# The attention scores' second product with the queries' high parts alone, the key blocks on two halves of the array's rows

## The chip, the cores and the metric

The kernel runs on one core of a Trainium2 chip. A core has TensorE (PE, the matrix array; its weight loads are listed apart as PEld), VectorE (DVE), ScalarE (ACT), GpSimd (POOL) and SyncE (SP, which here only issues transfers), and 16 DMA engines. The metric is the device time of one execution in microseconds; less is better.

## The reference, cut to what matters

One layer of a diffusion backbone over 1024 latent tokens and 256 context tokens, 1024 wide: a token mixer (a gated recurrence beside grouped-query attention), then a mixture of 16 experts. The change is in the attention alone: 8 query heads of 64 numbers, 2 key heads, each shared by 4 query heads, 1280 keys.

```
xqa = apply_axial_rope(rms_norm(heads(xaq, 8), q_norm_g), cos, sin)      # queries, (1, 1024, 8, 64)
keys = jnp.concatenate([cka, xka], axis=1)                                # (1, 1280, 2, 64)
...
s = jnp.einsum("bqhgd,bkhd->bhgqk", qi, k) * 64 ** -0.5                   # one block of 128 queries
p = jax.nn.softmax(s, axis=-1)
o = jnp.einsum("bhgqk,bkhd->bqhgd", p, v)
```

## The kernel before

All matrix products are of float32 numbers, and each number is kept as two parts: a high part rounded to the width that the array multiplies (`fp32r`), and a low part, the rest. A product is then a sum of products of parts. `split` makes both parts, the high one on ACT (line 92) and the low one on DVE (line 93).

The instructions of PE stand in the order in which the program is written; those of the other engines and of SP's queue are put in order by a scheduler, which follows priorities. Each engine runs its own in order.

**The attention** (lines 709 to 933) goes over 16 pairs (t, g): a tile t of 128 queries and a key head g with its 4 query heads. For each pair, 24 steps put on PE, in turn: `turn` (line 801: a block of the probabilities of this pair is turned, 4 transposes on line 804, then split), `softmax` of one head of the next pair (line 776), some matmuls of independent work (`fill.run`: the gates' projections, later the first branch, lines 176 to 178), and `values` (line 809: two matmuls on line 814). So while one pair is turned and multiplied with the values, the next one's scores are made. The amount of independent work at each step is fixed when the program is written.

**The scores.** `q_vec(t)` (line 743) norms and rotates a tile of queries on DVE (the first two tiles) or POOL (the others), with tables `cq` and `sq` that stay on the chip, and `q_turn(t)` (line 763) puts them on the array's rows: a tile `QT[t, g]` holds for each head 128 rows, the 64 high parts and under them the 64 low parts. The keys `KT[g]` have the two parts side by side along the free dimension, each one twice on the rows: `KT[g][:, 0]` is the high parts on rows 0 to 63 and again on rows 64 to 127, `KT[g][:, 1]` the low parts in the same way. So one matmul over 128 rows with `KT[g][:, 0]` gives (high + low of the query) times the key's high part, and a second one with `KT[g][:, 1]` adds (high + low of the query) times the key's low part. The 1280 keys are three blocks of 512, 512 and 256 (`SEG`), so a head takes 6 matmuls over all 128 rows. Behind each block's second matmul DVE takes the block's maximum over the keys (line 788); behind the third, line 792 joins the three, and ACT makes the exponentials (line 795). There are three banks `s` for scores (`NS`).

At the start of the attention PE has 16 us of independent work by the program's own count (`F0`), then `q_turn(0)` and the first four heads, with 3.4 us of independent work (`F1`) after each.

After the attention come the two branches' products and the output projection (from line 937), the routing of tokens to experts (from line 1185) and the experts, whose weights stream in from memory.

Of the kernel before, what the change touches and what calls it, by code (L numbers as in the profile page):

```python
# [28 lines left out]
def view(t, off, dims):  # L29
    """The tile's partitions with free dimensions [stride, size] from element off on."""  # L30
    a = t if isinstance(t, bass.AP) else t[:]
    return bass.AP(tensor=a.tensor, offset=a.offset + off, ap=[list(a.ap[0])] + [list(d) for d in dims])
# [13 lines left out]
def _layer(tc, nc, top, A, out):  # L46
# [35 lines left out]
    def rsqrt(pool, ss, n, scale, name):  # L82
        """(ss * scale + eps) ** -0.5"""
        m = pool.tile([128, n], F32, name=name + "m", tag="rsm", bufs=4)
        nc.gpsimd.tensor_scalar(m, ss, scale, EPS, op0=OP.mult, op1=OP.add)
        r = pool.tile([128, n], F32, name=name, tag="rsr", bufs=4)
        nc.gpsimd.tensor_tensor(r, m, mhalf[:, :n], op=OP.pow)
        return r

    def split(hi, lo, src, eng=None):  # L90
        """hi: src rounded to the parts' width; lo: what is left (exact)."""
        nc.scalar.copy(hi, src)  # L92
        (eng or nc.vector).tensor_tensor(lo, src, hi.bitcast(F32), op=OP.subtract)  # L93
# [3 lines left out]
    class Fill:  # L97
        """Matmuls of independent work, emitted between the steps of a dependent chain: the time is the tensor engine's."""
# [27 lines left out]
        def flushed(self):  # L126
            """The PSUM bank is on its way out: no matmuls into it for some steps."""
            self.wait = self.pause
# [7 lines left out]
    class Stream:  # L136
        """The weight chunks of the first sub-layer in the order of their use; each is loaded one chunk ahead."""
# [18 lines left out]
    def wload(src, kt, ncols, rowlen, off, hl=None):  # L156
        """A chunk of a weight: kt row tiles of 128, ncols columns from off on; as hi and lo."""
        raw = wp.tile([128, 2048], F32, name="raw", tag="raw", bufs=1)
        if not hl:
            hl = [wp.tile([128, 2048], F32R, name="w" + x, tag="w%s%d" % (x, nw[0] % 2)) for x in ("hi", "lo")]  # L160
            nw[0] += 1
        hi, lo = hl
        f = lambda t: t.rearrange("p (k c) -> p k c", k=kt)
        nc.sync.dma_start(f(raw), dram(src, off, [[rowlen, 128], [128 * rowlen, kt], [1, ncols]]))
        split(f(hi), f(lo), f(raw))
        return f(hi), f(lo)
# [5 lines left out]
    def mm3g(p, a, b, nk, first=True, last=True):  # L172
        """p += sum over k of a[k].T @ b[k]; a, b: pairs of functions of k giving the hi and lo parts."""
        for k in range(nk):
            s, e = first and k == 0, last and k == nk - 1
            nc.tensor.matmul(p, a[0](k), b[0](k), start=s, stop=False)  # L176
            nc.tensor.matmul(p, a[0](k), b[1](k), start=False, stop=False)  # L177
            nc.tensor.matmul(p, a[1](k), b[0](k), start=False, stop=e)  # L178
            yield 3 * p.shape[-1] / 2400

# [8 lines left out]
    # the tokens, halves of them apart: [half][hi, lo]  # L189
# [15 lines left out]
    def natural(hi, lo, emit, tiles):  # L205
        """Token rows on the partitions: emit(token tile, PSUM); ctx tiles are 0, 1, x tiles 2 to 9."""
        n = hi.shape[2]
        for t in tiles:
            h = HC if t < 2 else HX[(t - 2) // 4]
            o = (t if t < 2 else (t - 2) % 4) * 128  # L210
            p = pjt()
            yield from mm3g(p[:, :n], (lambda k: h[0][:, k, o:o + 128], lambda k: h[1][:, k, o:o + 128]),
                            (lambda k: hi[:, k], lambda k: lo[:, k]), 8)
            emit(t, p[:, :n])
            fill.flushed()

    def transposed(hi, lo, m, emit, ctx, halves=(0, 1)):
        """Features on the partitions: emit(first token, number of tokens, PSUM)."""
# [23 lines left out]
    with ExitStack() as st:  # L242
# [11 lines left out]
        # token tile t is loaded, normalised and transposed beside these row tiles of w_mod (9: after them)  # L254
# [51 lines left out]
        # rows 0, 1: the products with the hi parts of silu(c), silu(c_ctx); rows 2, 3: with the lo parts  # L306
# [64 lines left out]
    def rope_swap(o, x, s, eng):  # L371
        """o = x with the halves of each axis exchanged, times s; [128, heads, 64] each."""
        for i in range(2):
            u = lambda a, j: a.rearrange("p h (a f) -> p h a f", a=2)[:, :, :, j * 16:j * 16 + 16]
            eng.tensor_tensor(u(o, i), u(x, 1 - i), u(s, i), op=OP.mult)

    def gain_rows(rows, n):
        """A head's gains on all partitions, and the same with the halves of each axis exchanged."""
# [8 lines left out]
    lbp = consts.tile([128, 2, 4], F32, name="lbp")  # L387
    lb1 = consts.tile([128, 2, 4], F32, name="lb1")
    with ExitStack() as st:
        pool = st.enter_context(mkpool("right", name="sa", bufs=2))  # L390
        pps = st.enter_context(mkpool(name="saps", bufs=1, space=PSUM))
        # lower bounds: a softmax over the two layers' logits, its first component
# [19 lines left out]
        # keys: norm, rotary embedding; values as they are  # L412
# [63 lines left out]
        # the other adaLN parameters, as one row  # L476
# [33 lines left out]
        # their sums over the partitions, piece j of 512 on row j  # L510
# [20 lines left out]
    with ExitStack() as st:  # L531
# [41 lines left out]
        for i in range(2):  # L573
            for c in range(4):
                # of the last chunk the first half of the tokens first: it makes room
# [53 lines left out]
        def states(h, K, Z, acc, tt):  # L629
# [17 lines left out]
            def advance(d, i0, cs, kt):  # L647
# [3 lines left out]
                for i, c in enumerate(cs):  # L651
# [4 lines left out]
                    else:  # L656
                        # the state before the next chunk
# [51 lines left out]
    sOA = spill.tile([4, 128, T], F32, name="sOA")  # L709
    sBA = spill.tile([8, 128, T], F32, name="sBA")  # L710
    BA, BR, direct = [], [], [None]
# [6 lines left out]
    with ExitStack() as st:  # L718
# [15 lines left out]
        cq = pool.tile([128, 8, 64], F32, name="cq")  # L734
        sq = pool.tile([128, 8, 64], F32, name="sq")
        for i, (n, a) in enumerate((("c_cos", cq), ("c_sin", sq))):
            nc.scalar.dma_start(a, A[n].rearrange("(t p) c -> p t c", p=128))
            (nc.gpsimd, nc.vector)[i].tensor_tensor(a, a, rows[:, i:i + 1].to_broadcast([128, 8, 64]), op=OP.mult)
        QT, SC = {}, {}
# [3 lines left out]
        def q_vec(t):  # L743
            eng = nc.vector if t in QV else nc.gpsimd
            x = pool.tile([128, 8, 64], F32, name="aq", tag="aq")
            nc.sync.dma_start(x, sAQ[t].rearrange("p (h d) -> p h d", h=8))
            a = pool.tile([128, 8, 64], F32, name="qa", tag="qa")
# [8 lines left out]
            eng.tensor_tensor(a, x, cq[:, t:t + 1].to_broadcast([128, 8, 64]), op=OP.mult)  # L756
            rope_swap(b, x, sq[:, t:t + 1].to_broadcast([128, 8, 64]), eng)
# [14 lines left out]
        PT, SU = {}, {}  # L772
# [3 lines left out]
        def softmax(t, g, h):  # L776
            if h == 0:
                SU[t, g] = pool.tile([128, 3, 4], F32, name="su", tag="su", bufs=3)
            m = pool.tile([128, 8], F32, name="m", tag="m", bufs=3)
# [3 lines left out]
            for a, (c0, n, _) in enumerate(SEG):  # L783
                s = ps.tile([128, 512], F32, name="s", tag="s", bufs=NS)[:, :n]
                for i in range(2):
                    nc.tensor.matmul(s, QT[t, g][:, h], KT[g][:, i, c0:c0 + n], start=(i == 0), stop=(i == 1))  # L786
                with tc.high_priority(offset=HP):
                    nc.vector.tensor_reduce(m[:, a:a + 1], s, axis=AX.X, op=OP.max)  # L788
                ss.append(s)
            hp = tc.high_priority(offset=HP)  # L790
# [59 lines left out]
        def branch_in():  # L850
            """The first half of the tokens makes room for the first branch's input."""
# [90 lines left out]
    with ExitStack() as st:  # L942
# [4 lines left out]
        # the router on x1: its weights take the norm's gain and the scale; the shift gives a row  # L947
# [21 lines left out]
        # merged branches: [hi, lo][row tiles 0-3, 4-7][tokens 0-511, 512-1023]  # L969
# [95 lines left out]
        def y_part(t, c, nc_):  # L1065
            """x1 = x + g1 * y, quarters c, ... of the columns; their part of the mean square."""
# [49 lines left out]
        def spread(t):  # L1116
            """Tile t's affinities with (expert, copy) on the partitions: ar, and the top halves of the words in ar16."""
# [16 lines left out]
        def after(t, c):  # L1134
            """What follows the matmuls of quarter c of tile t."""
# [44 lines left out]
    with ExitStack() as st:  # L1180
        pool = st.enter_context(mkpool(name="tk", bufs=1))
        ps = st.enter_context(mkpool(name="tkps", bufs=1, space=PSUM))
        # token numbers and gates as exact parts
# [7 lines left out]
        # bits of the threshold from the top, 3 a round: the first 4 rounds on the words' top halves as numbers;  # L1191
        # float32 numbers hold the threshold exactly for 8 rounds, the last 6 bits are put in as bits
# [62 lines left out]
        # counted from 1: the rank among the larger, and after all of those the rank among the equal  # L1255
# [12 lines left out]
    with ExitStack() as st:  # L1268
# [39 lines left out]
        def chunk(src, e, n, kh):  # L1308
# [4 lines left out]
            # the low half goes where an earlier chunk came from  # L1313
# [28 lines left out]
        with tc.high_priority(offset=1000):  # L1342
            route(0)
            # the tensor engine stays busy, and its clock up, while the first tokens are gathered
# [6 lines left out]
        for e in range(16):  # L1351
# [36 lines left out]
            # the last expert meets the other experts' sums on chip; the final norm follows tile by tile  # L1388
# [106 lines left out]
```

## Time and profile before

| | us |
|---|---|
| median of 3 runs | 1856.06 (1855.23 to 1858.42) |
| span of the profiled execution | 1854.5 |
| PE busy in the span | 1731.6 (93%) |
| DVE busy | 1331.0 (72%) |
| ACT busy | 995.4 (54%) |
| POOL busy | 273.7 (15%) |

The span runs from the first instruction to the last one of the profiled execution; the median lies 1.6 us above it. Times inside the program are given in microseconds from the span's start. A matmul's record is longer than the time until the next one can start, because matmuls follow each other in a pipeline; so the cost of one on PE is read from the distance of two starts, and PE's busy time is an upper bound. A form such as `24*128` behind MATMUL or LDWEIGHTS is the size of the weights, rows by columns. The attention is the stretch from about 633 us to 1012 us.

### The profile page before, as it was taken

To read this page: it belongs to the slowest core of one execution; us is meant where nothing else is said; L and a number is where in the kernel's file an instruction comes from. 1 tells how busy PE (TensorE), PEld (TensorE's weight loads), DVE (VectorE), ACT (ScalarE), POOL (GpSimd) and SP (SyncE) were. 2 spreads that over 40 slices of the span, in tenths; PEclk is the share of its full clock that TensorE was granted. 3 is DMA by queue.
4 is the path that set the end of the run, shared out by engine and by line. 5 is a ranking of instruction groups with operands and counts; after the bars stand their busy time and mean duration, and the time that the engine had idled before them with its cause. 6 is when DMAs were issued, how large, how long until landed. Compare 5 with 4: busy or idle time off the path is not lost. (4 is left out here: it accounts for less than half of the span.)

```text
span 1854.5 us, 26192 instructions
## 1 busy us (share of the span) xinstructions
PE 1731.6 (93%) x9820; PEld 1454.9 (78%) x9820; DVE 1331.0 (72%) x2000; ACT 995.4 (54%) x1632; POOL 273.7 (15%) x241
## 2 busy tenths in 40 slices
PE   5899999999999799999999999939999999999995
PEld 2798887899988678787787788828888888887774
DVE  6656323876766466777875664469999999998897
ACT  6422331322323367777876532227777777777665
POOL 3400001020000201111100332140011001001103
PEclk9899999999999999999999999959999999999998
DMA  8285445353332410101212776459999999999972
GB/s 326 93 309 208 171 140 198 106 174 103 103 117 81 130 43 29 46 29 58 89 51 87 261 262 238 159 187 358 378 379 371 379 379 374 376 379 379 370 261 101
DMA packets 206319, 383.87 MB, mean 207 GB/s; under 512 B 17488, under 2 KB 65568, under 8 KB 202864
## 3 DMA queue, kind: packets, MB, share of 16 engines
q1 hardware_dynamic: 194944, 360.92, 54.4%
q0 software_dynamic: 4832, 19.34, 3.8%
q10 hardware_dynamic: 6416, 1.94, 0.4%
q8 instruction: 77, 1.26, 0.3%
q14 instruction: 50, 0.41, 0.1%
HBM read 323.02 MB, written 59.13 MB: 206 GB/s over the span
## 5 line engine op out<-in xcount | busy, mean ns | idle before, releaser
L93 DVE TENSOR_TENSOR elo<-eraw,ehi 128x1024 fp32r<-128x1024 f32 x378 | 452.2, 1221 | 22.2 <-ACT ehi L92 14.4
L92 ACT CAST ehi<-eraw 128x1024 fp32r<-128x1024 f32 x384 | 383.6, 1047 | 86.6 <-PE pgu L178 48.5
L177 PE MATMUL pgu<-elo,xeT 128*128 128x512 f32 x512 | 203.7, 398 | 2.8 <-DVE elo L93 2.4
L176 PE MATMUL pgu<-ehi,xeT 128*128 128x512 f32 x512 | 204.9, 400 | 0.2 <-ACT xeT L92 0.2
L178 PE MATMUL pgu<-ehi,xeT 128*128 128x512 f32 x512 | 202.4, 395 | 0.0
L176 PE MATMUL pj<-hx,whi 128*128 128x512 f32 x448 | 185.4, 414 | 6.5 <-ACT stg L69 5.3
L178 PE MATMUL pj<-hx,wlo 128*128 128x512 f32 x448 | 175.8, 392 | 0.0
L177 PE MATMUL pj<-hx,whi 128*128 128x512 f32 x448 | 175.5, 392 | 0.0
L795 ACT ACTIVATE p<-s,m,qsc 128x512 f32<-128x512 f32 (+1 forms) x192 | 134.3, 713 | 17.7 <-DVE m L792 17.5
L788 DVE TENSOR_REDUCE m<-s 128x1 f32<-128x512 f32 (+1 forms) x192 | 104.3, 596 | 48.5 <-PE s L786 48.2
L176 PE MATMUL pj<-whi,hx 128*128 128x256 f32 x448 | 130.9, 292 | 3.6 <-DVE stg L541 1.9
L92 ACT CAST pT<-ptp 128x512 fp32r<-128x512 f32 x160 | 92.7, 595 | 71.9 <-PE ptp L804 71.8
L178 PE MATMUL pj<-whi,hx 128*128 128x256 f32 x448 | 128.1, 286 | 1.4 <-DVE hx L93 1.3
L93 DVE TENSOR_TENSOR pT<-ptp,pT 128x512 fp32r<-128x512 f32 x160 | 108.3, 685 | 29.2 <-ACT pT L92 28.5
L177 PE MATMUL pj<-wlo,hx 128*128 128x256 f32 x448 | 127.4, 284 | 0.0
L177 PEld LDWEIGHTS pgu<-elo,xeT 128*128 128x128 f32 x512 | 96.3, 188 | 29.0 <-DVE elo L93 8.0
L176 PEld LDWEIGHTS pgu<-ehi,xeT 128*128 128x128 f32 x512 | 96.9, 189 | 21.8 <-ACT xeT L92 0.5
L178 PEld LDWEIGHTS pgu<-ehi,xeT 128*128 128x128 f32 x512 | 96.2, 188 | 22.6 <-DVE xeT L93 0.4
L1385 POOL DMA_INDIRECT ACC<-ye,idx x15 | 34.7, 2316 | 474.9 <-DVE ye L1384 474.9
L176 PE MATMUL pye<-ehi,hdT 128*128 128x512 f32 x256 | 104.8, 409 | 0.0
L177 PE MATMUL pye<-elo,hdT 128*128 128x512 f32 x256 | 102.1, 399 | 1.2 <-DVE elo L93 1.2
L814 PE MATMUL pv<-pT,vs 128*128 128x512 f32 x320 | 102.2, 403 | 0.9 <-DVE pT L93 0.8
(365 smaller groups left out, 3919.7 us busy)
## 6 DMA issues: line engine op xcount, KB each, us to landing
eraw<-in_w_exp_gate SPq DMA_DIRECT2D x64, 1024.0 KB, 12.0
eraw<-in_w_exp_up SPq DMA_DIRECT2D x64, 1024.0 KB, 11.6
eraw<-in_w_exp_down SPq DMA_DIRECT2D x64, 1024.0 KB, 12.2
wm<-in_w_mod SPq DMA_DIRECT2D x24, 1024.0 KB, 6.9
raw<-in_w_in SPq DMA_DIRECT2D x21, 1024.0 KB, 6.1
sFK<-sg SPq DMA_DIRECT2D x32, 256.0 KB, 2.3
sGT<-stg SPq DMA_DIRECT2D x32, 256.0 KB, 2.1
sgm<-sGT SPq DMA_DIRECT2D x32, 256.0 KB, 3.8
```

Source lines behind the costliest of these rows:

```text
L92: nc.scalar.copy(hi, src)
L93: (eng or nc.vector).tensor_tensor(lo, src, hi.bitcast(F32), op=OP.subtract)
L176: nc.tensor.matmul(p, a[0](k), b[0](k), start=s, stop=False)
L177: nc.tensor.matmul(p, a[0](k), b[1](k), start=False, stop=False)
L178: nc.tensor.matmul(p, a[1](k), b[0](k), start=False, stop=e)
L788: nc.vector.tensor_reduce(m[:, a:a + 1], s, axis=AX.X, op=OP.max)
L795: nc.scalar.activation(p, ss[a], AF.Exp, bias=m[:, 7:8], scale=sc, accum_out=SU[t, g][:, a, h:h + 1])
L814: nc.tensor.matmul(PV[t, g].rearrange("p a b -> p (a b)"), VS[:, g, j], hl[i], start=(j == 0 and i == 0), stop=(j == 9 and i == 1))
L1385: nc.gpsimd.indirect_dma_start(out=ACC, out_offset=bass.IndirectOffsetOnAxis(ap=idx[:, :1], axis=0), in_=ye, in_offset=None, compute_op=OP ...
```

## The change

The second product (the key's low parts) keeps the queries' high parts alone; the queries' low part times the key's low part is left out. It then has 64 rows in place of 128. The first two key blocks' second products are put on different halves of the array's rows: block 0 on rows 0 to 63, block 1 on rows 64 to 127, one right behind the other. Block 2 takes rows 0 to 63 by itself. For block 1 the queries' high parts must lie on rows 64 to 127: a new tile `Q2[t, g]` gets them from `QT[t, g]` by a transfer of 128 KB on SP's queue, one for each of the 16 pairs. In the built program the 192 second products are matmuls over half the rows (64 by 128), 128 of them at row 0 and 64 at row 64; the 192 first products stay at 128 by 128.

The room for `Q2` comes from the rotary tables: they are no longer kept on the chip. They are scaled as before, written to a table `sRT` in memory once, and `q_vec(t)` loads its 128 rows of both (`cs`, 64 KB) each time.

```diff
+    sRT = spill.tile([8, 128, 2, 64], F32, name="sRT")
...
-        cq = pool.tile([128, 8, 64], F32, name="cq")
-        sq = pool.tile([128, 8, 64], F32, name="sq")
-        for i, (n, a) in enumerate((("c_cos", cq), ("c_sin", sq))):
+        for i, n in enumerate(("c_cos", "c_sin")):
+            a = pool.tile([128, 8, 64], F32, name="rt", tag="pT1", bufs=3)
             nc.scalar.dma_start(a, A[n].rearrange("(t p) c -> p t c", p=128))
             (nc.gpsimd, nc.vector)[i].tensor_tensor(a, a, rows[:, i:i + 1].to_broadcast([128, 8, 64]), op=OP.mult)
+            nc.sync.dma_start(sRT[:, :, i].rearrange("t p c -> p t c"), a)
...
+            cs = pool.tile([128, 2, 64], F32, name="cs", tag="cs")
+            nc.sync.dma_start(cs, sRT[t])
...
-            eng.tensor_tensor(a, x, cq[:, t:t + 1].to_broadcast([128, 8, 64]), op=OP.mult)
-            rope_swap(b, x, sq[:, t:t + 1].to_broadcast([128, 8, 64]), eng)
+            eng.tensor_tensor(a, x, cs[:, :1].to_broadcast([128, 8, 64]), op=OP.mult)
+            rope_swap(b, x, cs[:, 1:].to_broadcast([128, 8, 64]), eng)
...
+                Q2[t, g] = pool.tile([128, 4, 128], F32, name="q2", tag="q2", bufs=2)
+                nc.sync.dma_start(Q2[t, g][64:], QT[t, g][:64].bitcast(F32))
...
-                for i in range(2):
-                    nc.tensor.matmul(s, QT[t, g][:, h], KT[g][:, i, c0:c0 + n], start=(i == 0), stop=(i == 1))
-                with tc.high_priority(offset=HP):
-                    nc.vector.tensor_reduce(m[:, a:a + 1], s, axis=AX.X, op=OP.max)
+                nc.tensor.matmul(s, QT[t, g][:, h], KT[g][:, 0, c0:c0 + n], start=True, stop=False)
                 ss.append(s)
+                if a == 0:
+                    continue
+
+                for b in ((0, 1) if a == 1 else (2,)):
+                    c1, n1, _ = SEG[b]
+                    r = slice(64, 128) if b == 1 else slice(0, 64)
+                    nc.tensor.matmul(ss[b], (Q2[t, g][r, h].bitcast(F32R) if b == 1 else QT[t, g][r, h]), KT[g][r, 1, c1:c1 + n1], start=False, stop=True)
+                    with tc.high_priority(offset=HP):
+                        nc.vector.tensor_reduce(m[:, b:b + 1], ss[b], axis=AX.X, op=OP.max)
```

The order on PE at the first head before (buffer numbers kept, so that the three banks `s` can be told apart):

```order
L769 MATMUL ptq_5507<-identr_78,qs_5409 128x128 x4
L786 MATMUL s_5515<-kT_5353,qT_5499 128x512 x2
L786 MATMUL s_5519<-kT_5353,qT_5499 128x512 x2
L786 MATMUL s_5523<-kT_5353,qT_5499 128x256 x2
L176 MATMUL pj_5543<-hx_83,whi_5275 128x512
```

The same place now; line 791 is the first product, over 128 rows, and line 799 the second, over 64:

```order
L773 MATMUL ptq_5512<-identr_78,qs_5414 128x128 x4
L791 MATMUL s_5522<-kT_5354,qT_5504 128x512
L791 MATMUL s_5524<-kT_5354,qT_5504 128x512
L799 MATMUL s_5522<-kT_5354,qT_5504 128x512
L799 MATMUL s_5524<-kT_5354,q2_5519 128x512
L791 MATMUL s_5530<-kT_5354,qT_5504 128x256
L799 MATMUL s_5530<-kT_5354,qT_5504 128x256
L176 MATMUL pj_5550<-hx_83,whi_5275 128x512
```

Both first products of the 512-key blocks now stand ahead of their second ones, and each head goes from 128 rows to 64, back to 128, to 64 and back to 128 for what follows.

The order on DVE ahead of the first scores before (`qa`, `qb` and `qs` are the queries' working tiles, `qT` is `QT`, `wlo` the low part of a weight chunk for the independent work):

```order
L738 TENSOR_TENSOR sq<-sq,rows 128x512
L375 TENSOR_TENSOR qb<-aq,sq 128x16x16 x2
L758 TENSOR_TENSOR qa<-qa,qb 128x512
L93 TENSOR_TENSOR qs<-qa,qs 128x8x64
...
L770 CAST qT<-ptq 128x512 x2
L788 TENSOR_REDUCE m<-s 128x1 x3
L93 TENSOR_TENSOR wlo<-raw,whi 128x2048
```

The same place now:

```order
L739 TENSOR_TENSOR rt<-rt,rows 128x512
L760 TENSOR_TENSOR qa<-aq,cs 128x512
L375 TENSOR_TENSOR qb<-aq,cs 128x16x16 x2
L762 TENSOR_TENSOR qa<-qa,qb 128x512
L93 TENSOR_TENSOR wlo<-raw,whi 128x2048
L93 TENSOR_TENSOR qs<-qa,qs 128x8x64
L375 TENSOR_TENSOR qb<-aq,cs 128x16x16
L752 TENSOR_TENSOR qa<-aq 128x512
L375 TENSOR_TENSOR qb<-aq,cs 128x16x16
L774 CAST qT<-ptq 128x512 x2
```

The split of a weight chunk has moved from behind the first maxima to ahead of the first queries' split, and the product with the cosines has moved behind the scaling of the tables.

SP's queue now, from the write of the tables to the transfers for tile 1 (`q_...` are the tiles `Q2`; the rows of `sGT` write finished independent work):

```order
L740 DMA sRT<-rt 128x8x64 x2
L70 DMA sGT<-stg 128x512
L750 DMA cs<-sRT 128x128
L748 DMA aq<-sAQ 128x512
L750 DMA cs<-sRT 128x128
L70 DMA sGT<-stg 128x512
L164 DMA raw<-in_w_in 128x8x256
L784 DMA q_5519<-qT 64x512
L784 DMA q_5718<-qT 64x512
L748 DMA aq<-sAQ 128x512
L750 DMA cs<-sRT 128x128
L70 DMA sGT<-stg 128x512 x3
```

The two transfers for `Q2` of tile 0 stand behind a load of a weight chunk, which itself has to wait for the split of the chunk before.

## Rows read from the trace of the kernel before

**Rows 1.** The page: the span of the profiled execution.

```profile
span 1854.5 us, 26192 instructions
```

**Rows 2.** Stretches: busy us of PE, PEld, DVE, ACT, POOL (instructions); PEclk, DMA share, GB/s.

```profile
657.00:1012.00 355.00, 347.88 (x1942) 282.90 (x1941) 259.95 (x585) 261.62 (x620) 37.44 (x38) 1.00 0.16 52
1200.00:1260.00 60.00, 29.86 (x154) 21.03 (x154) 41.29 (x99) 19.40 (x28) 21.61 (x15) 0.69 0.64 232
1260.00:1800.00 540.00, 536.33 (x2492) 429.45 (x2491) 508.65 (x561) 397.83 (x447) 59.58 (x29) 1.00 1.02 364
```

**Rows 3.** PE's waits from 655 to 1010 us: total us, times, longest us.

```profile
PE ptp L804 <- DVE pT L93: 2.8, 3, 1.7
...
PE pv L814 <- ACT pT L92: 0.2, 1, 0.2
```

**Rows 4.** A tile's instructions: first weight transfers of the experts (`eraw`); first and last start.

```profile
L1318 SPq DMA_DIRECT2D eraw<-in_w_exp_gate x12: 367/382/834, 1083.0 to 1283.9; - x12
```

**Rows 5.** Order of time: a head's six score matmuls; start us, us.

```profile
647.68 1.34 PE L786 MATMUL s<-kT,qT 128*128 128x512 f32 x6
...
648.86 0.39 PE L176 MATMUL pj<-hx,whi 128*128 128x512 f32 x1
...
649.09 0.39 PE L177 MATMUL pj<-hx,whi 128*128 128x512 f32 x1
```

**Rows 6.** Order of time: a matmul of 24 rows amid matmuls of 128.

```profile
1026.81 0.39 PE L178 MATMUL pb<-br,wlo 128*128 128x512 f32 x1
1027.13 0.13 PEld L958 LDWEIGHTS pvc<-ident,hd 24*128 24x128 f32 x1 [0.35 <-issue]
1027.13 0.24 PE L958 MATMUL pvc<-ident,hd 24*128 24x24 f32 x1
1027.29 0.19 PEld L176 LDWEIGHTS pb<-br,whi 128*128 128x128 f32 x1
...
1027.63 0.40 PE L177 MATMUL pb<-br,whi 128*128 128x512 f32 x1
```

**Rows 7.** Order of time: a matmul of 16 rows amid matmuls of 128.

```profile
125.43 0.28 PE L177 MATMUL pj<-wlo,hx 128*128 128x256 f32 x1
...
125.55 0.28 PE L178 MATMUL pj<-whi,hx 128*128 128x256 f32 x1
...
125.76 0.23 PE L399 MATMUL pl<-ident,lg 16*128 16x16 f32 x1
...
126.14 0.28 PE L177 MATMUL pj<-wlo,hc 128*128 128x256 f32 x1
```

**Rows 8.** Order of time: four transposes of 128 rows amid matmuls of 128.

```profile
760.33 0.63 PE L814 MATMUL pv<-pT,vs 128*128 128x512 f32 x2
...
760.79 0.60 PE L804 MATMUL ptp<-ident,p 128*128 128x128 f32 x4
...
761.46 0.39 PE L177 MATMUL pj<-hx,whi 128*128 128x512 f32 x1
```

**Rows 9.** Order of time: the way to the first scores.

```profile
623.11 0.69 DVE L738 TENSOR_TENSOR sq<-sq,rows 128x512 f32<-128x512 f32 x1
...
628.06 1.91 ACT L92 CAST whi<-raw 128x2048 fp32r<-128x2048 f32 x1 [2.09 <-PE pj L177]
628.10 0.79 PE L769 MATMUL ptq<-identr,qs 128*128 128x128 f32 x8
...
633.62 2.50 PE L786 MATMUL s<-kT,qT 128*128 128x512 f32 x6 [4.73 <-DVE qT L770]
...
635.92 0.63 PE L176 MATMUL pj<-hx,whi 128*128 128x512 f32 x1
...
636.67 2.28 DVE L93 TENSOR_TENSOR wlo<-raw,whi 128x2048 fp32r<-128x2048 f32 x1
```

**Rows 10.** Transfers issued from 600 to 660 us: count, KB each, median us to landing.

```profile
sGT<-stg SPq DMA_DIRECT2D x7, 256.0 KB, 3.2
...
cq<-in_c_cos ACTq DMA_DIRECT2D x1, 256.0 KB, 5.8
```

More of the change, by code (lines that the diff above doesn't have):

```diff
@@ L770, in q_turn @@
                 nc.vector.tensor_copy(QT[t, g], p.bitcast(F32))
-        PT, SU = {}, {}
+        PT, SU, Q2 = {}, {}, {}
         SEG = ((0, 512, 5), (512, 512, 6), (1024, 256, 7))
```

## The prediction

> **What bounds the kernel now.** I read the page first, then each engine's busy time stretch by stretch, then PE's waits inside the attention, and last the records in order of time. The profiled execution spans 1854.5 us [rows 1]. In the attention's steady part, 355 us from 657 to 1012, PE is busy for 348 us at full clock, DVE and ACT for 260 and 262, and the DMA engines for a sixth of the time [rows 2]. PE's own waits there, five groups in all, add up to 6.6 us [rows 3]. So in this stretch the matmuls, one behind the other, set the pace, and the other engines have a quarter of their time free. What follows starts when the attention ends: the last stages before the experts are short of something else (from 1200 to 1260 us PE is half idle while tokens are chosen), and from 1260 us on the DMA engines are busy all the time [rows 2]. The first transfer of an expert's weights is only issued at 1083 us [rows 4], 70 us after the attention, once the stages between have left room for it, so it moves with the attention's end: a microsecond more or less of PE in the attention is one of the whole program.
>
> **What the scores cost now.** Each of the 64 heads takes four matmuls of 512 columns and two of 256. Two starts of 512-column matmuls lie 0.23 us apart, and the whole group of six takes from 647.68 to 648.86, 1.18 us [rows 5]. In the second product 64 of the 128 rows carry the part that the change leaves out, but a matmul's time goes by its columns; so leaving them out saves nothing by itself. What can be saved is that the second products of blocks 0 and 1 run at the same time on two halves of the rows: at best one 512-column matmul a head, 0.227 us, 64 x 0.227 = 14.5 us.
>
> **What a change of the row size costs.** The new order goes 128, 128, 64, 64, 128, 64 rows and back to 128 for what follows: four changes of size a head, 256 in all. The trace of before has hardly any matmul with fewer rows, but two of them stand amid dense work. The first has 24 rows. Matmul L178 starts at 1026.81, and the next one of 128 rows that has its normal distance again starts at 1027.63, with one 128-row matmul and the small one in between [rows 6]: 0.82 us where two distances of 0.227 us make 0.45. The small one with its two changes has cost 0.37 us. The second has 16 rows: 0.59 us from 125.55 to 126.14, where two distances of 0.12 us (125.43 to 125.55) make 0.24, so 0.35 us [rows 7]. [...] By contrast, four 128-row transposes between 128-row matmuls cost only 0.44 us in all: from 760.33 to 761.46 are 1.13 us, of which three distances of 0.227 us are the big ones', so 0.11 us for each [rows 8]. A small matmul is not dear, then; the change of size is: the weights are loaded in the open.
>
> For one change this gives bounds. If the small matmul would have cost 0.11 us anyway, two changes cost 0.25 us, 0.125 each. If its own columns count for nothing (16 or 24 of them are 0.01 us), it is 0.18 each. The weights of 24 rows were loaded in 0.13 us and those of 128 rows in 0.19 [rows 6], and 64-row ones may take as long as 128-row ones, which would add 0.03 a change: 0.21 at the top. I take 0.18, since beside matmuls of 256 and 512 columns, whose load was hidden before, all of it comes into the open. Neither row shows 64 rows; I take them to behave like 24 and 16.
>
> [...]
>
> **The pair.** The second one's weights are loaded behind the first one's, 0.11 us later by the distance of the transposes [rows 8]. So of the 0.227 us I take 0.12 as saved; the bounds are 0.227 (both start together) and 0 (one after the other).
>
> **The sum on PE.** A head: 4 x 0.18 - 0.12 = +0.60 us; 64 heads: +38.4 us. The bounds: 4 x 0.125 - 0.227 = +0.27, or +17.5 us, and 4 x 0.21 - 0 = +0.84, or +54 us.
>
> **What the slower PE takes back.** The 6.6 us of waits [rows 3] are for ACT and DVE; if every head gives them 0.6 us more, part of it goes. I take 3 us off (0 to 6.6).
>
> **The start of the attention.** Before, the sine table is ready on the chip at 623.80, the queries are turned from 628.10 on, and the first scores start at 633.62 after PE has waited 4.73 us for DVE's copy [rows 9]. Now the tables go to memory and one tile of them comes back. Nearest rows: a write of 256 KB takes 3.2 us to land, and the table's own load, in pieces as short as the new write's, 5.8 us [rows 10]. I take 3.2 to 5.8 for the write and 3.2 for the read back, after which the product with the cosines, two with the sines and the sum follow on DVE (2.2 us, at 0.69 us each 128x512). Then DVE's new order puts the split of a weight chunk, 2.28 us [rows 9], ahead of the queries' split; the split (0.7), the turn (0.8) and the copy (0.7) follow. With 5.8: 623.8 + 5.8 + 3.2 + 2.2 + 2.3 + 2.2 = 639.5; with 3.2: 636.9. The first scores come 3.3 to 5.9 us later. Behind this, the first head's matmul on rows 64 to 127 waits for its transfer (3.2 us at most, some 2 of them behind the three matmuls ahead of it), and all of PE waits with it. So +5.3 to +7.9; I take 6.5. After the wait of before, the matmuls ran at the lower of the two clock levels for some microseconds (0.63 us long instead of 0.39 [rows 5, 9]); a longer wait falls in the same stretch, and I add nothing.
>
> **What costs nothing, and under which cover.** The other 15 transfers for `Q2` are issued some 48 matmuls, about 8 us, before their first use, more than twice what the transfer takes; uncovered it would be 15 x 3.2 = 48 us. Ahead of each on SP's queue stand writes of work that PE has finished earlier. The maxima of block 0 come about half a microsecond later, as do the exponentials; a head's probabilities are turned several steps later, and DVE and ACT have a quarter of their time free [rows 2]. The tables' eight small loads go with the queries' own, a tile ahead.
>
> **Sum.** 38.4 - 3 + 6.5 = +41.9 us on 1854.5, which is 1896.4 for a profiled execution. The median of the runs lies 1.6 us above the span, so 1898 us.
>
> **The rivals.**
>
> 1. *The two halves cost nothing to enter, and the pair runs together.* Then each head saves up to 0.227 us: 64 x 0.227 = 14.5 us, less the start's 6.5: 1848 us, faster. This decides if a change costs less than (0.227 - 6.5/64)/4 = 0.03 us. Against it stand both places of [rows 6, 7]; for it, that they show 24 and 16 rows alone, never 64. Chance 0.10. If in this case the second of the pair starts 0.11 us after the first, the saving is 7.5 us and the start eats it: no change, 0.03.
>
> [...]
>
> 2. *The weights are loaded during the change.* [...] Against it: both loads of [rows 6] start late. Chance 0.08.
>
> 3. *The clock.* With four more gaps a head PE's granted clock, 1.00 in the whole stretch [rows 2], could fall at times. Each 10 us at half clock cost 5; with a tenth of the stretch, 35 us, it is 18 us more, 1916 us. Against it: at [rows 9] it took a wait of almost 5 us. Chance 0.04.
>
> 4. *The pair doesn't do what it says* and runs one after the other: +0.12 us a head, 1906 us; this lies in the forecast's own range.
>
> **Chances and range.** My forecast, slower by its own bounds (1872 to 1918), gets 0.75. With rivals 2 and 3, slower by more than 0.2% (what a measurement of this kernel can just tell from no change) has 0.87, faster 0.10, same 0.03. For 8 in 10 the range is 1868 to 1918.
>
> **What the changed profile would show.** Right: the six matmuls of a head take about 1.8 us in place of 1.18; each weight load that follows a change of rows starts some 0.1 us after the matmul before it has gone through, not together with it; the two 64-row matmuls start about 0.11 us apart; the attention's steady part has grown from 355 to about 390 us with PE still the engine that doesn't wait; the first scores start at 637 to 640 us, and the first matmul on the upper rows waits for a transfer. Wrong: a head's group takes less than 1.1 us (rival 1) or about 1.35 (rival 2); or the later `Q2` transfers are waited for, to be seen as waits of the 64-row matmuls on a DMA.

## The result and the profile after

The changed kernel takes 1915.49 us (median of 4 runs, 1911.23 to 1917.79); the kernel before took 1856.42 beside it (1855.23 to 1858.42). The ratio is 1.0314, 95% interval 1.0301 to 1.0327: 59 us slower, where 42 were forecast. The profiled execution is the quickest of the four, and its span has grown by less than the medians, by 54.9 us [rows 1].

The page of the kernel after: its span and the engines' busy time.

```profile
span 1909.4 us, 26257 instructions
PE 1778.5 (93%) x9819; PEld 1458.0 (76%) x9820; DVE 1331.2 (70%) x2000; ACT 996.3 (52%) x1632; POOL 271.9 (14%) x241
```

DVE and ACT do the work that they did; only PE has become busier, by 47 us.

The attention's steady part, from the first turned block (L816) to the last product with the values (L826), in the view by stretches; the second row is the same part of the kernel before, cut in the same way. The columns are those of [rows 2].

```profile
666.20:1065.07 398.87, 385.38 (x1935) 281.10 (x1933) 261.06 (x583) 262.23 (x618) 37.27 (x38) 0.98 0.16 52
```

```profile
657.53:1011.06 353.53, 346.41 (x1935) 281.77 (x1934) 259.60 (x583) 261.52 (x618) 37.44 (x38) 1.00 0.16 52
```

With the same 1935 matmuls it lasts 398.9 us in place of 353.5, which is 45.3 of the 54.9 us. The granted clock has fallen from 1.00 to 0.98 on the mean. Nearly all the rest lies ahead of it: the steady part begins 8.7 us later.

A head's six score matmuls after, in order of time (the answer to [rows 5]):

```profile
765.68 0.30 PEld L791 LDWEIGHTS s<-kT,qT 128*128 128x128 f32 x2
765.71 0.71 PE L791 MATMUL s<-kT,qT 128*128 128x512 f32 x2
...
766.35 0.18 PEld L799 LDWEIGHTS s<-kT,qT 64*128 64x128 f32 x1 [0.36 <-issue]
766.35 0.50 PE L799 MATMUL s<-kT,qT 64*128 64x512 f32 x1
766.35 0.18 PEld L799 LDWEIGHTS s<-kT,q 64*128 64x128 f32 x1
766.35 0.49 PE L799 MATMUL s<-kT,q 64*128 64x512 f32 x1
...
766.78 0.38 PE L791 MATMUL s<-kT,qT 128*128 128x256 f32 x1
767.09 0.18 PEld L799 LDWEIGHTS s<-kT,qT 64*128 64x128 f32 x1
767.09 0.38 PE L799 MATMUL s<-kT,qT 64*128 64x256 f32 x1
...
767.40 0.42 PEld L816 LDWEIGHTS ptp<-ident,p 128*128 128x128 f32 x4
```

Two things are to be seen. Every weight load behind a change of rows begins together with its own matmul (766.35, 767.09, 767.40) and not under the one before; ahead of the first one PEld has stood idle for 0.36 us. And the pair's two loads and two matmuls all begin at 766.35. From 765.71 to 767.40 are 1.69 us, against 1.18 before [rows 5]: 0.51 us a head.

PE's waits over the steady part after (total, times, longest), to set against the 6.6 us of [rows 3]:

```profile
PE s L791 <- ACT p L807: 9.0, 18, 2.4
PE ptp L816 <- ACT p L807: 1.8, 1, 1.8
PE ptp L816 <- DVE pT L93: 1.4, 2, 0.7
PE pj L176 <- ACT stg L69: 0.7, 3, 0.3
PE pv L826 <- DVE pT L93: 0.2, 1, 0.2
```

They have not shrunk but doubled, to 13.1 us. Most of them, 9.0 us, are waits of the first product (L791) until the exponentials (L807) have given a bank of scores back. Before, this group had 1.7 us:

```profile
PE s L786 <- ACT p L795: 1.7, 4, 0.7
```

One such wait after, ACT and PE in order of time:

```profile
769.67 0.59 ACT L92 CAST pT<-ptp 128x512 fp32r<-128x512 f32 x1
...
770.87 1.26 POOL L762 TENSOR_TENSOR qa<-qa,qb 128x512 f32<-128x512 f32 x1
...
772.16 0.62 ACT L92 CAST qs<-qa 128x512 fp32r<-128x512 f32 x1 [1.90 <-POOL qa L762]
772.69 0.77 ACT L807 ACTIVATE p<-s,m,qsc 128x512 f32<-128x512 f32 x1
...
773.45 0.77 ACT L807 ACTIVATE p<-s,m,qsc 128x512 f32<-128x512 f32 x1
773.60 0.29 PEld L791 LDWEIGHTS s<-kT,qT 128*128 128x128 f32 x1 [2.61 <-ACT p L807]
773.60 1.55 PE L791 MATMUL s<-kT,qT 128*128 128x512 f32 x2 [2.38 <-ACT p L807]
```

ACT has the cast of the next tile's queries (`qs`) ahead of a head's exponentials and waits 1.90 us for POOL with it; the exponentials come late, no bank is free, and PE stands for 2.38 us. Before, the scheduler had put the same cast behind the exponentials, those of 21 heads against 20 now:

```profile
752.07 0.57 ACT L795 ACTIVATE p<-s,m,qsc 128x256 f32<-128x256 f32 x1
752.52 0.21 ACT L795 ACTIVATION_READ_ACCUMULATOR p<-s,m,qsc 128x1 f32 x1
753.29 0.62 ACT L92 CAST qs<-qa 128x512 fp32r<-128x512 f32 x1 [0.56 <-POOL qa L758]
```

After, two of the six tiles that POOL prepares meet this, and each time the granted clock then falls. The stretches around the wait shown:

```profile
773.00:774.00 1.00, 0.40 (x1) 0.29 (x1) 0.84 (x2) 1.00 (x3) 0.33 (x1) 0.62 0.16 46
774.00:775.00 1.00, 1.00 (x2) 0.29 (x1) 0.23 (x1) 1.00 (x5) 0.74 (x1) 0.50 0.00 0
```

The clock stays at 0.50, the lower of the two levels that whole slices show (the other is 1.00), until 780; the second time from 879 to 886. Summed over slices of 1 us, what it lacks to 1.00 in the steady part is 6.8 us, and nothing before.

The start, in order of time (to [rows 9]):

```profile
630.12 0.69 DVE L760 TENSOR_TENSOR qa<-aq,cs 128x512 f32<-128x512 f32 x1 [4.88 <-DMA cs<-sRT]
...
632.13 2.29 DVE L93 TENSOR_TENSOR wlo<-raw,whi 128x2048 fp32r<-128x2048 f32 x1
...
636.95 1.22 PE L791 MATMUL s<-kT,qT 128*128 128x512 f32 x2 [0.61 <-DVE qT L774]
...
641.34 0.79 PE L799 MATMUL s<-kT,q 64*128 64x512 f32 x1 [2.45 <-DMA q<-qT]
...
643.08 0.79 PE L176 MATMUL pj<-hx,whi 128*128 128x512 f32 x1
```

The first scores start at 636.95 in place of 633.62, and the first matmul on the upper rows waits 2.45 us for `Q2`. The independent work behind the first head begins at 643.08, against 635.92 [rows 9]: 7.2 us. The lower clock (0.50) lasts from 633 to 646 us here, before from 632 to 639.

### The profile page after: what moved, and what is told of

It is laid out like the page before. It is cut to its first block, busy times and chain, and to the rows that moved or that the text cites. A ratio compares the mean times of both kernels' runs of the same rounds, so it can differ in the third digit from the quotient of the medians.

```text
span 1909.4 us, 26257 instructions
## 1 busy us (share of the span) xinstructions
PE 1778.5 (93%) x9819; PEld 1458.0 (76%) x9820; DVE 1331.2 (70%) x2000; ACT 996.3 (52%) x1632; POOL 271.9 (14%) x241
## 5 line engine op out<-in xcount | busy, mean ns | idle before, releaser
L176 PE MATMUL pj<-hx,whi 128*128 128x512 f32 x448 | 189.5, 423 | 6.0 <-ACT stg L69 4.6
L177 PE MATMUL pj<-hx,whi 128*128 128x512 f32 x448 | 176.6, 394 | 0.0
L807 ACT ACTIVATE p<-s,m,qsc 128x512 f32<-128x512 f32 (+1 forms) x192 | 134.1, 711 | 11.4 <-DVE m L804 11.2
L826 PE MATMUL pv<-pT,vs 128*128 128x512 f32 x320 | 104.2, 410 | 0.2 <-DVE pT L93 0.2
L176 PEld LDWEIGHTS pj<-hx,whi 128*128 128x128 f32 x448 | 85.3, 190 | 25.0 <-ACT stg L69 6.7
L69 ACT COPY stg<-pj 128x512 f32<-128x512 f32 (+1 forms) x92 | 46.3, 503 | 110.3 <-PE pj L178 90.9
```

What stands on the lines that cost most here:

```text
L69: (eng or nc.scalar.copy)(x[:, :n], p)
L807: nc.scalar.activation(p, ss[a], AF.Exp, bias=m[:, 7:8], scale=sc, accum_out=SU[t, g][:, a, h:h + 1])
L826: nc.tensor.matmul(PV[t, g].rearrange("p a b -> p (a b)"), VS[:, g, j], hl[i], start=(j == 0 and i == 0), stop=(j == 9 and i == 1))
```

## The experiments

Two theories. *The change of rows*: the time is what four changes of row size a head cost, less the pair. *The new order*: with two first products ahead of any second one, two of three banks are taken before one is finished, and the engines behind get out of step; the halves cost little. Steady parts below are cut as above.

**1. The new order with all 128 rows** (`e1_full_rows`; no `Q2`), and **the tables alone** (`e4_tables`: the kernel before, with the diff's lines on `sRT` and `cs` only).

```diff
-                    nc.tensor.matmul(ss[b], (Q2[t, g][r, h].bitcast(F32R) if b == 1 else QT[t, g][r, h]), KT[g][r, 1, c1:c1 + n1], start=False, stop=True)
+                    nc.tensor.matmul(ss[b], QT[t, g][:, h], KT[g][:, 1, c1:c1 + n1], start=False, stop=True)
```

> The changed order and the tables in memory stay, but every second product goes over all 128 rows again (the low-times-low part is back, and there is no transfer for Q2). Theory, the changes of row size cost about 0.2 us each: a head's six matmuls are back at 1.18 us, the attention's steady part at 355 us plus some waits for banks, and what is left over before is the later start, 3 to 5 us: 1859 to 1866 us. Rival, the order of the six matmuls (two banks taken before the first is finished) and the slower clock stretches make most of the loss: still above 1885 us.

> The kernel before with the rotary tables in memory as the only change. Theory, the later start costs what the way through memory and the moved split take: first scores 3.3 us later, 1859 to 1861 us. Rival, it is hidden or the scheduler's order makes it good: 1856 us.

Measured: the new order 1873.06 us, ratio 1.0094 (1.0073 to 1.0114); the tables 1860.22, ratio 1.0028 (1.0014 to 1.0042); before 1855.34. So the tables cost 5 us, all ahead of the steady part (353.6 us, as before), and the order alone costs 12.8 us more, with no matmul changed in size. Its steady part:

```profile
659.68:1028.29 368.61, 353.43 (x1934) 286.05 (x1933) 258.55 (x584) 262.06 (x618) 37.43 (x38) 0.99 0.15 51
```

That is 15.0 us longer than with the tables alone. The same two stalls are in it (PE waits 2.38 us at 759.13 for the exponentials). The tables' time is as the theory had it; the new order's lies between the ranges of its two theories, so neither holds by itself.

**2. The pair and the changes, one at a time in the new order.** `e2_two_changes` gives block 2's second product all 128 rows, so two changes a head are left; `e3_no_pair` puts block 1 on rows 0 to 63 too, without `Q2`.

```diff
-                    r = slice(64, 128) if b == 1 else slice(0, 64)
+                    r = (slice(0, 64), slice(64, 128), slice(0, 128))[b]      # e2_two_changes
+                    r = slice(0, 64)                                          # e3_no_pair, all on QT
```

> Only the third block's second product goes over 128 rows again (with its low-times-low part), so that a head has two changes of row size in place of four; the pair stays. Theory, 0.2 us a change: 128 changes fewer are 26 us less than the changed kernel, 1887 to 1893 us. Rival, a matmul over 64 rows is slow in itself or the pair is what costs: at most 8 us less, above 1905 us.

> The second products of blocks 0 and 1 both go to rows 0 to 63, so they can't run at the same time; no Q2 and no transfer for it; four changes a head as in the changed kernel. Theory, the pair does run at the same time in the changed kernel: 0.21 us a head more, 14 us, less the first head's wait for its transfer of 2.5 us, so 1924 to 1930 us. Rival, the pair runs one after the other anyway and the records' equal starts mislead: 1911 to 1916 us.

Measured: with two changes 1889.27 us, ratio 1.0194 (1.016 to 1.0228); without the pair 1925.19, ratio 1.0377 (1.0347 to 1.0407). Between ratios, two changes less are 1.2% of 1856 us, 22 us for 128 changes: 0.17 us each. Their steady part is 377.2 us, 21.7 less than after, over the 60 heads in it: 0.18 us each, or 0.15 without the 3.4 us that the clock alone gives back there (it lacks 3.4 us in place of 6.8). Without the pair the steady part is 413.0 us, 14.1 more: 0.235 us a head, of which up to 0.03 is a clock that lacks 1.7 us more there. Both times are as their theories had them. The head without the pair, in order of time:

```profile
770.52 0.73 PE L797 MATMUL s<-kT,qT 64*128 64x512 f32 x2
771.18 0.38 PE L789 MATMUL s<-kT,qT 128*128 128x256 f32 x1
```

On the same half the two take 0.66 us until the next matmul starts, on two halves 0.43 (766.35 to 766.78 above). The pair saves 0.23 us, one whole 512-column matmul: over 64 rows the second one on the same half takes as long as one over 128 rows (0.23 [rows 5]). That is less than the four changes cost, so the first theory holds for the halves; but experiment 1 shows the second one at work beside it.

**3. Changes in the old order.** `e7_two_on_before` and `e8_six_on_before` put 64-row second products into the kernel before, with nothing else changed: for block 2 alone, or for all three.

```diff
-                    nc.tensor.matmul(s, QT[t, g][:, h], KT[g][:, i, c0:c0 + n], start=(i == 0), stop=(i == 1))
+                    r = slice(0, 64) if a == 2 and i == 1 else slice(0, 128)     # e7; e8: slice(0, 64) if i == 1
+                    nc.tensor.matmul(s, QT[t, g][r, h], KT[g][r, i, c0:c0 + n], start=(i == 0), stop=(i == 1))
```

> The kernel before, with nothing changed but the third block's second product, which goes over rows 0 to 63 (its low-times-low part is left out): two changes of row size a head, no pair, no transfer, the old order. Theory, 0.2 us a change whatever stands around it: 128 x 0.2 = 26 us more, 1880 to 1883 us. Rival, a change is dear only together with the new order or the transfers: under 1870 us. If the matmul's time went by its rows, it would be below 1855 us.

> The kernel before with all three second products over rows 0 to 63 (low-times-low left out): six changes of row size a head, the old order. Theory, the cost goes by the number of changes: 384 x 0.2 = 77 us more, 1928 to 1936 us. Rival, changes that lie close together overlap, or other engines' free time hides part of it: under 1915 us.

Measured: 1877.71 us, ratio 1.0112 (1.0093 to 1.013), and 1921.78, ratio 1.0353 (1.0324 to 1.0383), before 1856.74. That is 21.0 us for 128 changes and 65.0 for 384: 0.164 and 0.169 us each, in proportion to their number. Both times are 2 to 6 us below the theory's ranges, which went by 0.2 us, and above the rivals'. The six-change kernel's weight loads, in order of time, and all of PE's waits from 655 to 1080 us:

```profile
769.36 0.19 PEld L787 LDWEIGHTS s<-kT,qT 128*128 128x128 f32 x1
769.79 0.18 PEld L787 LDWEIGHTS s<-kT,qT 64*128 64x128 f32 x1 [0.24 <-issue]
770.22 0.19 PEld L787 LDWEIGHTS s<-kT,qT 128*128 128x128 f32 x1 [0.24 <-issue]
```

```profile
PE s L787 <- ACT p L796: 1.2, 2, 0.9
PE pj L176 <- ACT stg L69: 0.8, 3, 0.3
PE ptp L805 <- DVE pT L93: 0.6, 1, 0.6
```

Loads that lie 0.43 us apart, where two 512-column matmuls lie 0.23 apart [rows 5], make 0.20 us a change there. And in the old order the slower PE does take waits back: 6.6 us [rows 3] have become 2.6.

**4. The stalls on ACT.** `e5_pool_split` (on the changed kernel), `e6_rows_pool` (on experiment 1's new order) and `e9_before_pool` (on the kernel before) let POOL split the queries of tiles 2 to 7, so that ACT has no cast to wait with.

```diff
-            split(qs[:, :, 0], qs[:, :, 1], a)
+            if t in QV:
+                split(qs[:, :, 0], qs[:, :, 1], a)
+            else:
+                nc.gpsimd.tensor_copy(qs[:, :, 0], a)
+                nc.gpsimd.tensor_tensor(qs[:, :, 1], a, qs[:, :, 0].bitcast(F32), op=OP.subtract)
```

> The changed kernel, but from the third tile of queries on their high and low parts are made on POOL in place of ACT and DVE. In the changed kernel's trace ACT stands for 1.9 us at that split, twice with a head's exponentials queued behind it, so that PE waits 2.4 us for a bank of scores, and its clock falls for 6.8 us each time. Theory, that is part of what the prediction left out: 2 x 2.4 for the waits and 2 x 3.4 for the clock, so 10 to 13 us less than the changed kernel, 1902 to 1906 us. Rival, the waits for banks come from the new order of the matmuls alone: 1911 to 1916 us.

> The same move of the queries' split to POOL, made on the kernel with the changed order and tables but all second products over 128 rows (e1_full_rows, 1873 us). Theory: its two stalls go, 2 x 2.4 us and the clock's 2 x 1.7 us, so about 8 us less, 1863 to 1866 us; what is left above the tables' 1860 us is the order's own waits for banks. Rival: no change, 1873 us.

> The kernel before, with the queries' split of tiles 2 to 7 on POOL in place of ACT and DVE; nothing else. Theory (the split on ACT only costs where the new order has put it ahead of a head's exponentials; the old order has it behind them): no difference that can be measured, 1853 to 1858 us. Rival (the split on POOL is a gain of its own, of the size of 6.5 or 14.6 us that it brought in the other two kernels): 1842 to 1850 us; then those two gains would be no evidence for ACT's order.

Measured: the changed kernel 1900.87 us, ratio 1.0241 (1.022 to 1.0261); the new order 1866.53, ratio 1.005 (1.0035 to 1.0064); the kernel before 1856.22, ratio 0.9994 (0.9983 to 1.0005). So the split on POOL is worth nothing that can be measured in the old order, about 8 us (1.0094 less 1.005) in the new one and about 14 (1.0314 less 1.0241) in the changed kernel; in steady parts 8.6 us (to 360.0) and 9.2 (to 389.6). The first two times miss the theories' ranges by about 1 us or less; both lie outside the rivals'. The long waits and the fall of the clock are gone in both. What is left of the order is 6.4 us of steady part, and this of PE's waits:

```profile
PE s L793 <- ACT p L809: 5.8, 19, 1.0
PE ptp L818 <- DVE pT L93: 2.9, 3, 1.5
```

Nineteen short waits for a bank, where the kernel before had 1.7 us of them in its 6.6. The profile's waits are 3.5 us more than before, but what they cost is more than they show. A head with such a wait, in order of time:

```profile
671.91 0.49 PE L793 MATMUL s<-kT,qT 128*128 128x512 f32 x1
672.67 0.50 PE L793 MATMUL s<-kT,qT 128*128 128x512 f32 x1 [0.27 <-ACT p L809]
673.00 0.63 PE L801 MATMUL s<-kT,qT 128*128 128x512 f32 x2
```

The second first product starts 0.76 us behind the first, where 0.23 is the distance without a wait. In 17 of the 60 heads a matmul of the group waits in this way, with the tables alone in 3; the other heads take 1.29 us on the mean in both kernels. All 60 groups, from the first score matmul to the next other matmul, take 86.2 us against 79.5: 6.7 us, so all of the 6.4 lies in heads that wait for a bank.

**5. A fourth bank.** If those short waits are the rest of the order's price, a fourth bank for scores must take it away. The bank has to come from the turned tiles, so the old order runs with the same banks beside it.

```diff
-    NS, NPT = 3, 3
+    NS, NPT = 4, 2
```

> The kernel with all second products over 128 rows, in the new order, tables in memory and the split on POOL, with four banks for scores and two for turned tiles (three and three before). To be compared with e11, which has the old order and the same banks. Theory (the order's last 6 us are waits for banks, since two first products hold two of three banks before either is finished): with a fourth bank the order costs 0 to 2 us against e11, and PE's waits for ACT's exponentials in front of s fall from 5.3 us to under 2. Rival (the order costs it in some other way, such as the later maxima and exponentials): 5 to 7 us against e11. The two banks for turned tiles may cost both kernels some microseconds.

> The control for e10: the old order of the six matmuls over 128 rows, tables in memory, split on POOL, four banks for scores and two for turned tiles. Both theories: 1856 to 1866 us, depending on what the third bank for turned tiles was worth; what counts is the difference of e10 from it.

> The changed kernel (64-row second products, the pair on the two halves) with the split on POOL and four banks for scores, two for turned tiles. Theory (changes of row size and pair +31 us, start +7): e11 plus 29 to 34 us, no more waits for the exponentials' banks: 1886 to 1896 us. Rival (the order's cost comes with the pair in another way): 1899 to 1903 us, as with three banks.

Measured: the new order 1917.97 us, ratio 1.0323 (1.0303 to 1.0344); the old one 1906.31, ratio 1.0267 (1.0248 to 1.0285); with the pair 1947.73, ratio 1.0487 (1.0466 to 1.0508). All three expectations missed, since going from three banks for turned tiles to two costs over 40 us. PE's waits from 655 to 1090 us in the new order:

```profile
PE ptp L818 <- DVE m L806: 19.0, 11, 3.8
PE ptp L818 <- DVE pT L93: 13.0, 11, 3.3
...
PE s L793 <- ACT p L809: 0.3, 1, 0.3
```

The waits for a bank of scores are gone (0.3 us), as the theory had it, but the turned tiles now wait for DVE, and the new order loses 10 to 12 us to the old one there. So by the total time this doesn't tell whether banks were the whole of the 6.4 us: it only shows that PE's short waits were for banks, and experiment 4 has what they cost. The changes and the pair cost the same here: 1.0487 less 1.0323 is 30 us.

## Why the prediction was right, and where its sum was off

The direction held, the time lies in the range, and the cause given, changes of row size, is the largest term. That it lies in the range is in part luck, for two terms missed in opposite directions, the pair's saving and the new order's cost: had the pair saved 0.12 us a head as forecast, the time would be some 7 us longer (64 x 0.11), 1922 us, outside the range. The spans' 54.9 us by the prediction's own steps:

- **A change of row size, 0.18 us.** Right. Experiment 2 gives 0.15 to 0.18; experiment 3 gives 0.164 and 0.169 with the waits taken back in it, and (60.3 + 4.0 - 1.7) / 360 = 0.17 without (the six-change kernel's steady part is 413.9 us, of which the clock lacks 1.7). 24 and 16 rows were a fair stand-in for 64. Rivals 1 and 2, a change that costs nothing or hides the load, fall: each load is seen in the open, at the start of its own matmul (766.35, 767.09). No run shows when a matmul's columns have gone through, nor the 0.1 us by which a load was to follow them, nor the term behind rival 2's 1.35 us a head; what the trace shows is a matmul that starts, behind a change, 0.43 us after a 512-column one (766.35 to 766.78) or 0.31 after a 256-column one (766.78 to 767.09), and 1.69 us for the head.
- **The pair, 0.12 us saved.** Too low: it saves 0.23, the upper bound. The second one's load does not come 0.11 us behind the first; they start at the same recorded time (766.35, in records of 10 ns). Rival 4 falls. The two terms make 4 x 0.18 - 0.23 = +0.49 a head, the head above shows 0.51, and the two kernels with POOL's split, which lose no clock, differ by 29.6 us over 60 heads, 0.49: about 32 us in all, not 38.4.
- **What the slower PE takes back, -3 us.** This step failed. It holds in the old order, where experiment 3 shows 4 us taken back. But the change also puts both first products ahead of the second ones, and this was costed only as maxima that come half a microsecond later, under cover. Experiment 1 measures the order alone at +12.8 us (15.0 in the steady part). Of this 8.6 are two long stalls, where ACT's new order has the queries' cast ahead of a head's exponentials, and the clock behind them; 6.4 are left, which lie in the 17 heads that wait for a bank (experiment 4). The cover, a quarter of ACT's time, was a mean: what counted was when a bank came free. The orders that the prediction rests on are those of PE, DVE and SP; ACT's, which had moved too, is not among them.
- **The start, +6.5 us.** Right in place and size: 7.2 us in the trace. The first scores come 3.3 us later, the low end of the forecast, the wait for the first `Q2` is 2.45, and the rest, 1.4, is a first head that takes 3.68 us beside its wait in place of 2.30, all of it at the lower clock. The start itself varies between kernels: the first scores are 5.4 us later with the tables alone and 3.7 in the new order with all 128 rows.
- **Nothing for the other 15 transfers.** Right: none of PE's waits in the steady part is for a transfer.
- **The clock, rival 3** (18 us, for more gaps in every head). The changes alone don't bring it down: with POOL's split the changed kernel keeps its 256 changes, and the granted clock of its steady part is 1.00 from slice to slice. In the changed kernel it fell behind the two long stalls, and that is at most 6.8 us. But a long stall is not needed: in the kernel without the pair it also fell at 917 and 1046 us, 2 to 3 us behind waits of 0.74 and 0.48 us, and in the six-change kernel at 784, 2 us behind one of 0.89, each time for 1.7 us of loss. Why there, when the kernel before has waits of up to 1.7 us without a fall, stays open.

The steady part's 45.3 us, as differences of steady parts: 9.2 for the two stalls and the clock behind them (the changed kernel less the same with POOL's split), 29.6 for the changes and the pair, 6.4 for the short waits of the new order, and 0.1 for the tables. With the start's 7.2 that is 52.5 of the spans' 54.9; of the rest 1.5 us lie between, where the other three of the first four heads stand (3 x 0.5), and 0.9 behind the attention. The medians differ by 4 us more than the spans, as the changed kernel's profiled execution was the quickest of the four; whether the stalls cost more in other executions stays open.

None of the versions with half-row products beats the kernel before: the pair can save 0.23 us a head, and even the two changes that it needs by itself cost 0.36.

## What to carry to other kernels

Two half-row matmuls side by side saved one whole matmul here (0.23 us, 512 columns), but a switch from 128 rows to 64 or back cost about 0.18 us, nearly that much: gather many halves behind one switch (no run here tries that), or leave them. When a change holds accumulators open longer, look at when each bank is given back and at the new order on every engine that gives one back, not at those engines' mean load. And price the rearrangement that a change needs by itself, in an experiment that has it and nothing else.

## What the runs showed that was not expected

The pair's loads and matmuls start within the 10 ns of the records (766.35), so the pair costs as one (0.43 us until the next matmul starts, against 0.66 on the same half). A wait of PE of 2.4 us was followed by 3.4 us at the lower clock level in the 128-row kernel (760 to 763) and 6.8 us in the changed one (773 to 780), though the same cast caused both; and waits of under 1 us were followed by a fall as well in two other kernels. And giving up the third bank for turned tiles costs over 40 us, more than the scores' order costs here.
